# Hybrid diffusion layers on one core: the first modulation as chunks on the tensor engine, two feature tiles in turn

## The chip, the cores and the metric

One core of a Trainium2 chip runs the whole program. The metric is the device time of one execution in microseconds (us). The engines: PE (tensor engine; PEld is its weight load), DVE (vector engine), ACT (scalar engine), POOL (GpSimd) and SP, which here only issues DMAs. Each engine works through its own queue in the order in which the program was scheduled, and waits for the others by semaphores.

## What is computed

Two layers of a diffusion backbone over 512 latent tokens and 256 context tokens, width 1024. Only the beginning of the first layer matters here:

```python
sh_a, sc_a, g_a, sh_f, sc_f, g_f = jnp.split(silu_c @ mod_w[l] + mod_b[l], 6, axis=-1)
csh_a, csc_a, cg_a, csh_f, csc_f, cg_f = jnp.split(silu_cc @ mod_w[l] + mod_b[l], 6, axis=-1)
a_lat = modulate(h_lat, sh_a, sc_a)        # rms_norm(x) * (1 + scale) + shift
a_ctx = modulate(h_ctx, csh_a, csc_a)
...
p_lat = a_lat @ w_in
p_ctx = a_ctx @ w_in
```

`silu_c` belongs to the latent tokens and `silu_cc` to the context tokens; both use the same `mod_w`. After this come attention, the output product and SwiGLU of layer 0, then layer 1 and a final norm. All of it is in float32; the large products split each operand into a rounded high part and a rest, and add three products (high x high, high x rest, rest x high).

## The kernel before, in words

Activations lie feature-major: `X[k]` holds feature tile k (128 of the 1024 features, one per partition) for 768 tokens, of which `LATS` are the first 512 and `CTXS` the last 256. A scheduler with a timeline of its own sets the order of instructions on each engine; the buffers per tag (`BUFS`, `PBUFS`) say how far loads run ahead (12 of `st`, 4 each of `ph` and `pl`, 3 each of `wr`, `wh` and `wl`).

The start of the program, up to about 92 us of the profile, does this:

- It loads `X` for the latent tokens (L157, eight DMAs of the SP queue), squares it (L348, ACT), adds the squares (L351, DVE), sums them over the partitions (L365, PE), takes root and reciprocal (L367 ACT, L368 DVE) and spreads the result over the partitions (L369 DVE, L374 PE, L377 ACT). That is `rms`; `r` is its result. The context tokens go through the same lines once more.
- Component 1 (scale) of the modulation is made by PE in four chunks of 256 features, both token kinds at once (`mods_pe`): the weights arrive as four tiles of 128x512 per chunk, eight products give rows (L191), ACT copies them (L193), PE turns them into columns (L195), DVE adds the bias (L199).
- Component 0 (shift) is made tile by tile (`mod_tile`, its `dense` branch): for each of eight feature tiles two DMAs of 256 KB, two multiply-and-sum instructions by DVE for the latent tokens (L237, L241), and for the context tokens a product by POOL (L254), a sum by ACT (L255) and two small steps of DVE (L257, L258). These read the conditioning vector spread over the partitions, which `load_cond` loads (512 KB each) and puts through a SiLU on ACT (L163).
- For each feature tile, `modulate` forms x times scale times r (L399, DVE), adds the shift with rounding to the high part (L400, ACT) and forms the rest (L401, DVE). `load_start` loads the tile's weights (256 KB) and splits them (L340 ACT, L341 DVE). `start_products` (L751 to L753) adds the tile's share to six PSUM banks `ov`: four of latent tokens (three products each, so 12 matmuls) and two of context tokens (6 matmuls).
- `SCALES` says before which feature tile a chunk of the scale is made. The latent part of tile k comes first, then the context part of the tiles that are `late`.

Behind the start the banks are copied out (`put_vs`, L473 and L474), while PE goes on with the first panels of `w_in` (L316 to L318), and the modulation of component 2 runs in the background by the same `mod_tile` path.

Of the kernel before, what the change touches and what calls it, by code (L numbers as in the profile page):

```python
# [14 lines left out]
P = 128  # L15
# [34 lines left out]
NR = "nb"  # L50
PE_MODS = ((0, 1), (0, 4), (0, 5))
SCALES = (2, 0, 1, 0, 1, 0, 0, 0)
KEEP = 1
# [5 lines left out]
KC = (0, 1, 0)  # L59
C1 = 0  # L60
VP = 0
# [39 lines left out]
def hybrid_kernel(ctx: ExitStack, tc, I, out):  # L101
# [54 lines left out]
    for k in range(KT):  # L156
        dma(X[k][:, LATS], I["xc"][k, :, LATS])  # L157
    modb = const("modb", [P, 96])
# [15 lines left out]

    MOD, picks = {}, []

    dense, tile, late, first = [True], [-9], [], {}

    def mods_pe(l, comp, get):
# [4 lines left out]
        for c in range(4):  # L184
            o = get()
            for k in range(KT):
                if k % 2 == 0:
                    w = T("st", [P, 512]) if comp == 1 else T(("ph", "pl")[k // 2 % 2], [P, 512])
                    dma(w, I["mod_wp"][PE_MODS.index((l, comp)), c, k // 2])
                g = slice(32 * (k % 4), 32 * (k % 4) + 32)  # L190
                PE.matmul(o[g, :NX], cond_col[:, k], w[:, NX * (k % 2) : NX * (k % 2) + NX], start=k < 4, stop=k > 3)  # L191
            t, d = T("p", [P, NX]), get()
# [548 lines left out]
    r = B(tag="nb")  # L741
    rms(X, LATS, r, lambda: PS("t"))
    A = [(B(F32R), B(F32R)) for _ in range(KT)]
# [12 lines left out]
    def start_products(k, w, tiles):  # L756
        for t in tiles:
            three(ov[t], [x[:, t * P : (t + 1) * P] for x in A[k]], w, k == 0, k == KT - 1)

# [29 lines left out]

    scales, late = mods_pe(0, 1, PM), deque()  # L790
    for k in range(KT):
        for _ in range(SCALES[k]):
            next(scales)
        if k == 0:
            load_cond(0)
            if C1 == 0:
                load_cond(1)
        shift = mod_tile(0, 0, k, (0, 1))
        next(shift)
        modulate(A[k], X[k], k, r, 0, 0, 0, LATS)  # L800
        w = load_start(k)
        start_products(k, w, range(4))
        late.append((k, w, shift))
        if k == 0:
            if C1:
                load_cond(1)
            for x in range(KT):
                dma(X[x][:, CTXS], I["xc"][x, :, CTXS])
            rms(X, CTXS, r, lambda: PS("t"))
        while late:  # L810
            i, w, shift = late.popleft()
            next(shift)
            modulate(A[i], X[i], i, r, 0, 0, 1, CTXS)
            start_products(i, w, (4, 5))
    sel = const("sel", [4, P], F32R)
# [784 lines left out]
```

## Time and profile before

| | us |
|---|---|
| median of three runs | 1619.1 (1618.13 to 1621.35) |
| the profiled execution: its own time | 1621.04 |
| the profiled execution: span | 1619.3 |
| PE busy in the span | 1540.7 (95%) |
| DVE / ACT / POOL busy in the span | 1215.1 / 812.2 / 316.9 |
| PE busy in the first 92 us | 58.15 |
| DVE busy in the first 92 us | 74.24 |

Times in the rows are microseconds from the start of the span; a row of the timeline gives start, duration, engine, line, operation and what it writes and reads, and in brackets the idle time before it and what ended that. Rows of stretches give the stretch, its length, then busy time (and instructions) of PE, PEld, DVE, ACT and POOL, the granted PE clock (1.00 is full), the DMA engines' busy share and GB/s.

### The profile page before, as it was taken

How to read it: one execution, taken by the hardware profiler on the slowest of the kernel's cores; microseconds unless marked ns; L12 is line 12 of the kernel's file. 1: busy time of each engine (PE TensorE's matmuls, PEld its weight loads, DVE VectorE, ACT ScalarE, POOL GpSimd, SP SyncE). 2: the span in 40 equal slices, each digit the busy share in tenths (PEclk: the TensorE clock that was granted, in tenths of full speed). 3: DMA queues.
4: the chain of work that ended last, by engine and by line, in shares of the span. 5: the costliest groups of instructions: out<-in, count | busy, mean ns of one | idle time of the engine just before them, and what ended most of it. 6: DMA issues, size and time to landing. Idle time of an engine off the chain costs nothing. (4 is left out here: it accounts for less than half of the span.)

```text
span 1619.3 us, 26531 instructions
## 1 busy us (share of the span) xinstructions
PE 1540.7 (95%) x9906; PEld 1365.0 (84%) x9906; DVE 1215.1 (75%) x2438; ACT 812.2 (50%) x1652; POOL 316.9 (20%) x319
## 2 busy tenths in 40 slices
PE   4799989999998999999999999999999999999997
PEld 2577867786896999999999998787879998898997
DVE  5994868667678679596767777768877688687685
ACT  5453576677365324243333333467756554454453
POOL 1550733321000110202111112384003000000002
PEclk9999999999999999999999999999999999999998
DMA  9445232101752363646547477122005133223222
GB/s 330 160 163 169 60 118 84 36 11 28 246 196 93 114 209 124 234 153 208 200 144 270 163 254 261 60 92 79 1 1 185 50 112 122 93 92 118 91 99 85
DMA packets 77913, 214.92 MB, mean 133 GB/s; under 512 B 10196, under 2 KB 17880, under 8 KB 77784
## 3 DMA queue, kind: packets, MB, share of 16 engines
q1 hardware_dynamic: 60888, 147.16, 28.0%
q0 software_dynamic: 14592, 62.92, 11.2%
q10 hardware_dynamic: 2304, 3.15, 0.5%
q8 instruction: 78, 1.28, 0.3%
q14 instruction: 51, 0.42, 0.1%
HBM read 186.97 MB, written 23.07 MB: 130 GB/s over the span
## 5 line engine op out<-in xcount | busy, mean ns | idle before, releaser
L306 ACT CAST wh<-wr 128x1024 fp32r<-128x1024 f32 (+2 forms) x148 | 113.4, 781 | 204.1 <-PE pss L317 40.6
L307 DVE TENSOR_TENSOR wl<-wr,wh 128x1024 fp32r<-128x1024 f32 (+2 forms) x145 | 137.3, 954 | 80.2 <-ACT wh L306 79.8
L351 POOL TENSOR_TENSOR p<-p,p 128x256 f32<-128x256 f32 (+1 forms) x33 | 33.1, 1002 | 464.1 <-ACT p L348 463.1
L541 ACT ACTIVATE p<-p,sm 128x512 f32<-128x512 f32 (+3 forms) x144 | 105.1, 730 | 34.9 <-DVE sm L545 32.5
L215 DVE CUSTOM_DVE_ANT_0 p<-rope,cond 128x1024 bf16<-128x1024 f32 x64 | 77.2, 1222 | 34.1 <-DMA rope<-in_mod_w_dram 34.0
L317 PE MATMUL psd<-b,wh 128*128 128x512 f32 (+3 forms) x266 | 89.8, 339 | 0.1
L316 PE MATMUL psd<-b,wh 128*128 128x512 f32 (+3 forms) x226 | 80.1, 354 | 1.6 <-ACT b L474 1.0
L210 POOL DMA_DIRECT2D rope<-in_mod_w_dram x48 | 25.8, 537 | 284.9 <-DVE mod L215 284.9
L316 PE MATMUL pss<-st,wh 128*128 128x256 f32 (+2 forms) x233 | 79.2, 340 | 1.4 <-ACT st L1051 0.9
L535 PE MATMUL pso<-ph,b 128*64 128x256 f32 (+1 forms) x384 | 77.0, 359 | 3.3 <-DVE ph L473 3.3
L1239 PE MATMUL pss<-b,wh 128*128 128x256 f32 (+1 forms) x258 | 79.3, 307 | 0.7 <-ACT b L340 0.7
L1241 PE MATMUL pss<-b,wl 128*128 128x256 f32 (+1 forms) x258 | 79.3, 307 | 0.1
L1240 PE MATMUL pss<-b,wh 128*128 128x256 f32 (+1 forms) x258 | 79.4, 308 | 0.0
L318 PE MATMUL pss<-st,wl 128*128 128x512 f32 (+2 forms) x233 | 79.0, 339 | 0.0
L318 PE MATMUL psd<-b,wl 128*128 128x512 f32 (+3 forms) x226 | 78.3, 347 | 0.0
L535 PE MATMUL pso<-pl,b 128*64 128x256 f32 (+1 forms) x384 | 76.7, 359 | 0.2 <-DVE pl L473 0.2
L1239 PE MATMUL pst<-b,wh 128*128 128x384 f32 (+1 forms) x240 | 74.9, 312 | 0.0
L1240 PE MATMUL pst<-b,wh 128*128 128x384 f32 (+1 forms) x240 | 74.8, 312 | 0.0
L1241 PE MATMUL pst<-b,wl 128*128 128x384 f32 (+1 forms) x240 | 74.3, 311 | 0.0
L317 PE MATMUL pss<-b,wh 128*128 128x256 f32 (+3 forms) x228 | 73.2, 323 | 0.3 <-DVE b L1227 0.2
L1240 PE MATMUL psd<-b,wh 128*128 128x384 f32 (+1 forms) x222 | 69.8, 314 | 0.3 <-DVE b L341 0.3
L1239 PE MATMUL psd<-b,wh 128*128 128x384 f32 (+1 forms) x222 | 69.6, 314 | 0.0
(548 smaller groups left out, 5496.9 us busy)
## 6 DMA issues: line engine op xcount, KB each, us to landing
wr<-in_w_gu_dram SPq DMA_DIRECT2D x88, 512.0 KB, 3.9
rope<-in_mod_w_dram POOLq DMA_DIRECT2D x48, 512.0 KB, 3.8
wr<-in_w_out_dram SPq DMA_DIRECT2D x32, 512.0 KB, 3.6
wr<-in_w_dn_dram SPq DMA_DIRECT2D x64, 256.0 KB, 3.0
p<-home POOLq DMA_DIRECT2D x40, 384.0 KB, 5.3
home<-p POOLq DMA_DIRECT2D x40, 384.0 KB, 4.2
wr<-in_w_in_dram SPq DMA_DIRECT2D x21, 512.0 KB, 3.5
ph<-in_mod_w_dram SPq DMA_DIRECT2D x24, 256.0 KB, 3.4
```

The costliest lines, as they stand in the source:

```text
L215: V.tensor_tensor_reduce(out=T("p", [P, D], mybir.dt.bfloat16), in0=w, in1=cond[:, v, :], op0=ALU.mult, op1=ALU.add, scale=1.0, scalar=0.0 ...
L306: behind(S.copy(h, r), *after[:1])
L307: behind((G if eng else V).tensor_tensor(lo, r, f(h), op=ALU.subtract), *after[1:])
L316: PE.matmul(o, wh[:, k], mh[:, c], start=first and k == 0, stop=False)
L317: PE.matmul(o, wh[:, k], ml[:, c], start=False, stop=False)
L318: PE.matmul(o, wl[:, k], mh[:, c], start=False, stop=last and k == n - 1)
L351: marks["add"] = (eng or V).tensor_tensor(acc[:, :n], acc[:, :n], t[:, :n], op=ALU.add)
L535: ins = PE.matmul(o[64 * i : 64 * i + 64, c], v(kt), t, start=n == 0, stop=n == len(moving[i]) - 1)
L541: S.activation(p[:, c], p[:, c], AF.Exp, bias=nm, scale=-1.0, accum_out=dn)
L1239: PE.matmul(o, wh, xh, start=first and k == 0, stop=False, skip_group_check=not first)
L1240: PE.matmul(o, wh, xl, start=False, stop=False, skip_group_check=not first)
L1241: PE.matmul(o, wl, xh, start=False, stop=k == 3, skip_group_check=not first)
```

## The change

- Component 0 of layer 0 joins the components that PE makes in chunks, for both token kinds (`PE_MODS`). Its weights come from the chunk layout; chunks of scale and shift alternate (`first_mods`), two feature tiles per chunk pair. The per-tile work of DVE, POOL and ACT for this component is gone.
- `X` is loaded by the SP and the ACT queue in turn.
- The squares of the latent `X` are six by ACT and two by DVE; they are added in pairs, and PE adds the four pair sums (16 instructions instead of 4 at the line `sum`).
- The first tiles of `w_start` are split ahead of the loop. In the loop, the latent products of two tiles come first, then the next chunk of scale and of shift (held behind those products by `chunk_after`), then the context products of the two tiles. The context norm stands behind the second chunk pair.
- The context half of `X` is loaded in two groups of four; `load_cond` comes with the third pair.

```diff
--- before.py
+++ after.py
@@ -48,8 +48,7 @@
 QF = 0
 LQ, EACH = 50, 0
 NR = "nb"
-PE_MODS = ((0, 1), (0, 4), (0, 5))
-SCALES = (2, 0, 1, 0, 1, 0, 0, 0)
+PE_MODS = ((0, 1), (0, 0), (0, 4), (0, 5))
 KEEP = 1
 OUTQ = 1
 E1, EF = 1, 1
@@ -57,7 +56,6 @@
 AFTER = "012k5678"
 DBG = 0.38
 KC = (0, 1, 0)
-C1 = 0
 VP = 0
 TURN1, MANY = (0,), 0
 RK, RQ, RL, SQ = (2, 0), (0, 0), (0, 0), 1
@@ -154,7 +152,7 @@
     cond = T("cond", [P, 2, D])
     X = [B() for _ in range(KT)]
     for k in range(KT):
-        dma(X[k][:, LATS], I["xc"][k, :, LATS])
+        (nc.sync, nc.scalar)[k % 2].dma_start(X[k][:, LATS], I["xc"][k, :, LATS])
     modb = const("modb", [P, 96])
     ident_r = const("ident", [P, P], F32R)
 
@@ -172,7 +170,7 @@
     S.activation(cond_col, cond_col, AF.Silu)
 
 
-    MOD, picks = {}, []
+    MOD, picks, chunk_after = {}, [], []
 
     dense, tile, late, first = [True], [-9], [], {}
 
@@ -188,7 +186,8 @@
                     w = T("st", [P, 512]) if comp == 1 else T(("ph", "pl")[k // 2 % 2], [P, 512])
                     dma(w, I["mod_wp"][PE_MODS.index((l, comp)), c, k // 2])
                 g = slice(32 * (k % 4), 32 * (k % 4) + 32)
-                PE.matmul(o[g, :NX], cond_col[:, k], w[:, NX * (k % 2) : NX * (k % 2) + NX], start=k < 4, stop=k > 3)
+                behind(PE.matmul(o[g, :NX], cond_col[:, k], w[:, NX * (k % 2) : NX * (k % 2) + NX], start=k < 4, stop=k > 3),
+                       *chunk_after)
             t, d = T("p", [P, NX]), get()
             S.copy(t, o[:, :NX])
             for m in range(2):
@@ -739,7 +738,17 @@
 
 
     r = B(tag="nb")
-    rms(X, LATS, r, lambda: PS("t"))
+    squares = []
+    for k in range(KT):
+        t = B(tag="p")
+        if k in (5, 7):
+            V.tensor_tensor(t[:, LATS], X[k][:, LATS], X[k][:, LATS], op=ALU.mult)
+        else:
+            S.activation(t[:, LATS], X[k][:, LATS], AF.Square)
+        if k % 2:
+            V.tensor_tensor(t[:, LATS], t[:, LATS], squares[-1][:, LATS], op=ALU.add)
+        squares.append(t)
+    rstd(squares[1::2], D, LATS, r, lambda: PS("t"))
     A = [(B(F32R), B(F32R)) for _ in range(KT)]
 
     def load_start(k):
@@ -755,7 +764,8 @@
 
     def start_products(k, w, tiles):
         for t in tiles:
-            three(ov[t], [x[:, t * P : (t + 1) * P] for x in A[k]], w, k == 0, k == KT - 1)
+            ins = three(ov[t], [x[:, t * P : (t + 1) * P] for x in A[k]], w, k == 0, k == KT - 1)
+        return ins
 
     def project(src, use, cols=(LATS, CTXS), m=P, every=2, eng=None, w=None, get=PQ):
 
@@ -787,31 +797,35 @@
         turn[0] += 1
         return PS("ot"[turn[0] % 2])
 
-    scales, late = mods_pe(0, 1, PM), deque()
-    for k in range(KT):
-        for _ in range(SCALES[k]):
-            next(scales)
-        if k == 0:
-            load_cond(0)
-            if C1 == 0:
-                load_cond(1)
-        shift = mod_tile(0, 0, k, (0, 1))
-        next(shift)
-        modulate(A[k], X[k], k, r, 0, 0, 0, LATS)
-        w = load_start(k)
-        start_products(k, w, range(4))
-        late.append((k, w, shift))
-        if k == 0:
-            if C1:
-                load_cond(1)
-            for x in range(KT):
-                dma(X[x][:, CTXS], I["xc"][x, :, CTXS])
+    late = deque()
+    first_mods = [mods_pe(0, comp, PM) for comp in (1, 0)]
+
+    for g in first_mods:
+        next(g)
+    starts = [load_start(k) for k in range(2)]
+    for c in range(0, KT, 2):
+        for k in (c, c + 1):
+            modulate(A[k], X[k], k, r, 0, 0, 0, LATS)
+            gate = [start_products(k, starts[k], range(4))]
+        chunk_after[:] = gate
+        for i, g in enumerate(first_mods if c + 2 < KT else ()):
+            if c == 0:
+                for x in range(4 * i, 4 * i + 4):
+                    dma(X[x][:, CTXS], I["xc"][x, :, CTXS])
+            next(g)
+            if c + i == 0:
+                starts.extend(load_start(k) for k in (2, 3))
+        if c == 0:
             rms(X, CTXS, r, lambda: PS("t"))
-        while late:
-            i, w, shift = late.popleft()
-            next(shift)
-            modulate(A[i], X[i], i, r, 0, 0, 1, CTXS)
-            start_products(i, w, (4, 5))
+        elif c + 2 < KT:
+            starts.extend(load_start(k) for k in (c + 2, c + 3))
+        for k in (c, c + 1):
+            modulate(A[k], X[k], k, r, 0, 0, 1, CTXS)
+            start_products(k, starts[k], (4, 5))
+        if c == 4:
+            for v in range(2):
+                load_cond(v)
+    chunk_after.clear()
     sel = const("sel", [4, P], F32R)
     VN = [B() for _ in range(4)]
     sets = [(new_q(), new_k()) for _ in range(2)]
```

The lines of the changed kernel are shifted against those of the kernel before (by one or two lines up to the loop, by 9 or 14 behind). What stands in the queues now, at three places:

First, ACT at the norm of the latent tokens. `b_68` to `b_75` are the eight tiles of `X`, `pst` a bank, `sm` the small tile of the norm, `nb_97` is `r`, `wr`/`wh` are a tile of `w_start` and its high part. Before:

```order
L348 ACTIVATE p_118<-b_75 128x512
L147 CAST ident_r_88<-nb_86 128x128
L367 ACT_TABLE_LOAD
L367 ACTIVATE sm_122<-pst_121,eps_90 128x4
L377 COPY nb_97<-pst_131 128x512
L163 ACT_TABLE_LOAD
L163 ACTIVATE cond_67<-cond_67 128x1024
L193 COPY p_175<-pst_158 128x256
L163 ACTIVATE cond_67<-cond_67 128x1024
L193 COPY p_199<-pst_182 128x256
L340 CAST wh_227<-wr_225 128x512
```

With the change:

```order
L747 ACTIVATE p_108<-b_72 128x512
L747 ACTIVATE p_113<-b_74 128x512
L145 CAST ident_r_88<-nb_86 128x128
L339 CAST wh_219<-wr_217 128x512
L339 CAST wh_225<-wr_223 128x512
L366 ACT_TABLE_LOAD
L366 ACTIVATE sm_119<-pst_118,eps_90 128x4
L376 COPY nb_97<-pst_140 128x512
L339 CAST wh_291<-wr_289 128x512
L192 COPY p_184<-pst_167 128x256
L192 COPY p_210<-pst_193 128x256
```

Two casts of `w_start` now stand ahead of the root (`sm`) of the norm, one more behind it, and the two SiLUs of `cond` are gone from this place.

Second, ACT at the norm of the context tokens. Before:

```order
L348 ACTIVATE p_259<-b_71 128x256
L348 ACTIVATE p_262<-b_72 128x256
L255 ACTIVATE pl_216,part_288<-pl_216 128x512
L348 ACTIVATE p_265<-b_73 128x256
L348 ACTIVATE p_268<-b_74 128x256
L348 ACTIVATE p_271<-b_75 128x256
L340 CAST wh_318<-wr_316 128x512
L367 ACT_TABLE_LOAD
L367 ACTIVATE sm_275<-pst_274,eps_90 128x2
L340 CAST wh_391<-wr_389 128x512
L377 COPY nb_97<-pst_282 128x256
L400 ACTIVATE b_134<-p_293,mod_70_211 128x256
```

With the change (`p_322` is the copied row of the second chunk of the shift; `p_322` and `p_329` are different tiles of one tag):

```order
L192 COPY p_322<-pst_305 128x256
L347 ACTIVATE p_329<-b_68 128x256
L347 ACTIVATE p_331<-b_69 128x256
L347 ACTIVATE p_334<-b_70 128x256
L347 ACTIVATE p_337<-b_71 128x256
L347 ACTIVATE p_340<-b_72 128x256
L347 ACTIVATE p_343<-b_73 128x256
L347 ACTIVATE p_346<-b_74 128x256
L161 ACT_TABLE_LOAD
L161 ACTIVATE cond_67<-cond_67 128x1024
L347 ACTIVATE p_349<-b_75 128x256
L161 ACTIVATE cond_67<-cond_67 128x1024
```

All eight squares are now behind the copy of the second shift chunk. A table load and both SiLUs of `cond` stand ahead of the root of the norm, and behind these rows follow the cast of `sel`, a second table load, the root itself and the copy to `r`.

Third, PE around the third chunk pair (`pss`, `pst_162` are banks of latent tokens, `psd` of context tokens, `pst_439` of the shift chunk). With the change:

```order
L761 MATMUL pst_162<-wl_298,b_149 128x512
L762 MATMUL pst_162<-wh_297,b_150 128x512
L194 MATMUL pso_433<-pick_64,p_432 128x2 x2
L189 MATMUL pst_439<-ph_440,cond_col_63 32x256 x2
L189 MATMUL pst_439<-pl_444,cond_col_63 32x256 x2
L189 MATMUL pst_439<-ph_448,cond_col_63 32x256 x2
L189 MATMUL pst_439<-pl_452,cond_col_63 32x256 x2
L194 MATMUL pso_457<-pick_64,p_456 128x2 x2
L760 MATMUL psd_163<-wh_291,b_147 128x512
L761 MATMUL psd_163<-wl_292,b_147 128x512
L760 MATMUL psd_164<-wh_291,b_147 128x512
```

The chunk pair ends (the last row of `pick_64`) and the context products of the third feature tile (`b_147`) follow directly behind it. In the kernel before no shift stands on PE, and the context products of a tile follow the latent products of the next tile.

## Prediction

> **What bounds the kernel now.** I read the stretches first, to see which engine is full where.
>
> ```profile
> 0.00:92.00 92.00, 58.15 (x263) 40.93 (x264) 74.24 (x152) 49.15 (x108) 37.56 (x28) 0.93 0.70 237
> 92.00:140.00 48.00, 46.97 (x291) 40.56 (x289) 37.86 (x78) 26.11 (x58) 14.95 (x10) 1.00 0.44 141
> 80.00:90.00 10.00, 7.84 (x32) 5.53 (x31) 10.00 (x20) 4.61 (x13) 6.70 (x5) 1.00 0.57 193
> ```
>
> In the first 92 us PE (first number behind the length) is busy for 58 of 92 us; from 92 us on it is full. DVE (third number) is busy for 74 us, and in the last of these stretches it has no idle time at all. The change touches only this start, so I ask by how much the moment moves at which PE becomes full. That moment is read from these rows of the timeline:
>
> ```profile
> 26.09 0.80 PE L751 MATMUL pss<-wh,b 128*128 128x512 f32 x1 [3.02 <-ACT b L400]
> 81.08 0.39 PE L316 MATMUL pst<-b,wh 128*128 128x512 f32 x1
> 81.31 0.39 PE L317 MATMUL pst<-b,wh 128*128 128x512 f32 x1
> 91.41 0.61 PE L753 MATMUL psd<-wh,b 128*128 128x512 f32 x2
> 92.31 0.28 PE L316 MATMUL pss<-b,wh 128*128 128x256 f32 x1
> ```
>
> The first product starts at 26.09. Matmuls of 512 columns follow each other at 0.23 us (81.08 to 81.31). The last product of the start begins at 91.41, but the first panel of `w_in` (24 matmuls on `pst`) has run in its gaps since 81.08, so at 92.31 PE is past 144 products of the start and these 24. 92.31 is the mark that I compare.
>
> The longest wait of PE for another engine's products up to 95 us (sum, times, longest), and the costliest groups of DVE and POOL up to 110 us (busy, mean ns of one, idle before them):
>
> ```profile
> PE pss L753 <- DVE b L401: 6.2, 5, 1.6
> L237 DVE CUSTOM_DVE_ANT_0 p<-pl,cond,mod 128x512 bf16<-128x512 f32 x15 | 13.2, 878 | 0.1
> L254 POOL TENSOR_TENSOR ph<-ph,cond 128x512 f32<-128x512 f32 x15 | 24.9, 1659 | 38.5 <-ACT cond L163 21.1 <-DVE mod L237 14.2 <-DVE mod L199 1.2
> ```
>
> PE waits for the results of `modulate` (L400 in the row at 26.09, L401 here), which stand on DVE among the shift's sums. Taking the shift off DVE and POOL (16 of the 30 L237 and 16 of the 30 L254 in these groups and their twins) therefore removes the wait that holds PE now. The question is what comes late in its place.
>
> **The first norm and the first product.** ACT will hold two casts of `w_start` ahead of the norm's root. They wait for their tiles, which SP issues behind x, 48 and 64 KB of constants and eight modulation tiles. Bytes up to the second one: 18 times 256 KB, and 128, 48 and 64 KB, about 4.97 MB.
>
> ```profile
> 0.00:10.00 10.00, 0.00 (x0) 0.00 (x0) 2.99 (x6) 5.64 (x9) 0.32 (x5) 1.00 0.77 251
> 10.00:20.00 10.00, 6.31 (x42) 3.38 (x42) 2.94 (x5) 5.14 (x8) 0.00 (x0) 1.00 1.03 373
> 20.00:30.00 10.00, 5.55 (x23) 4.51 (x20) 8.78 (x22) 8.93 (x20) 3.35 (x2) 0.66 0.98 315
> 30.00:40.00 10.00, 5.61 (x51) 3.48 (x49) 7.59 (x15) 3.57 (x10) 3.23 (x2) 1.00 1.05 380
> 12.40 1.86 PE L365 MATMUL pst<-ones,p 128*128 128x1 f32 x8 [12.40 <-DVE p L351]
> 14.30 0.27 ACT L367 ACTIVATE sm<-pst,eps 128x4 f32<-128x4 f32 x1 [1.61 <-PE pst L365]
> 15.55 2.08 PE L374 MATMUL pst<-p,ones 128*128 128x512 f32 x2 [1.29 <-DVE p L369]
> 17.56 2.56 PE L191 MATMUL pst<-st,cond_col 128*32 128x256 f32 x32
> L340 ACT CAST wh<-wr 128x512 fp32r<-128x512 f32 x8 | 4.9, 612 | 2.5 <-DMA wr<-in_w_start_dram 1.6 <-PE psd L753 0.8
> ```
>
> The DMA engines move 2.51 MB by 10 us and are full from there at 373 GB/s, so the second tile lands at 10 + 2.46/0.373 = 16.6. Then cast 0.61 and table load 1.28 (a row below): 18.5, where the root stands at 14.30 now. From root to spread takes 1.25 (14.30 to 15.55), spread and two chunks run to 20.12 as now (4.57): 24.3. The new path then goes through PE's columns, a bias step, two tiles of scale, a bias step and ACT:
>
> ```profile
> 36.58 0.50 PE L195 MATMUL pso<-pick,p 128*128 128x2 f32 x4
> L199 DVE SCALAR_TENSOR_TENSOR mod<-pso,modb 128x2 f32<-128x2 f32 x8 | 1.0, 149 | 0.2 <-PE pso L195 0.2
> 50.73 0.74 DVE L401 SCALAR_TENSOR_TENSOR b<-p,mod,b 128x512 fp32r<-128x512 f32 x1
> 34.01 0.48 DVE L399 SCALAR_TENSOR_TENSOR p<-b,mod,nb 128x256 f32<-128x256 f32 x1
> L399 DVE SCALAR_TENSOR_TENSOR p<-b,mod,nb 128x256 f32<-128x256 f32 x8 | 11.0, 1374 | 0.0
> L400 ACT ACTIVATE b<-p,mod 128x512 fp32r<-128x512 f32 x8 | 5.8, 722 | 11.5 <-DVE mod L241 11.5
> L400 ACT ACTIVATE b<-p,mod 128x256 fp32r<-128x256 f32 x8 | 4.0, 501 | 5.9 <-DVE mod L258 5.0 <-DVE p L399 0.9
> ```
>
> The L399 of 256 columns takes 0.48 alone, and 1.37 in the mean of all eight, most of which overlap a product of POOL. POOL now stands idle until component 2 begins, so I take the short durations: 0.74 for 512 columns, as L401 at 50.73, which has the same operands' sizes, and 0.48 for 256. The sum is 0.5 + 0.3 + 1.5 + 0.3 + 0.7 and a tenth for handing on: first product at **27.7**, against 26.09. With stretched steps on DVE it would be 29, the upper end.
>
> Two edits I cost at nothing here. Two queues for x: the engines are full from about 5 us on, and the casts above wait for later bytes; without them ACT would have the root at about 16.4, since PE now adds four pair sums, 32 of its entries instead of 8 at 0.23 us from about 10 us on. So without this cover the edit would still be late by 2 us. The earlier add of squares is hidden in the same way.
>
> **Two tiles and the second chunk pair.** 24 matmuls at 0.23 us, of which the first run at half clock:
>
> ```profile
> 46.00:48.00 2.00, 0.79 (x2) 0.69 (x3) 2.00 (x5) 1.26 (x3) 0.10 (x1) 0.55 0.29 108
> 50.00:52.00 2.00, 2.00 (x6) 1.59 (x5) 2.00 (x8) 1.12 (x3) 1.12 (x1) 0.50 0.00 0
> 52.00:54.00 2.00, 2.00 (x8) 1.55 (x7) 2.00 (x6) 1.34 (x3) 0.72 (x2) 0.75 0.46 131
> 28.00:30.00 2.00, 2.00 (x8) 1.63 (x7) 1.76 (x6) 1.97 (x3) 0.00 (x0) 0.72 0.99 367
> 37.01 1.11 PE L191 MATMUL pst<-st,cond_col 128*32 128x256 f32 x16
> L193 ACT COPY p<-pst 128x256 f32<-128x256 f32 x4 | 1.4, 361 | 0.2 <-DVE mod L237 0.2
> ```
>
> The granted clock is about 0.5 from some 23 to 28.7 and from 46.5 to 53, each time until PE has been busy for 2.6 and 5.8 us. I take 3 us here: it holds 7 matmuls at twice 0.23, and 17 at 0.23 follow, 6.9 in all: 34.6. A chunk is 1.1 (L191), a copy 0.36, columns 0.5; two chunks in turn end at 38.6, the second copy at **38.1**.
>
> **The context norm.** Behind that copy ACT does everything that the context products need:
>
> ```profile
> 27.17 1.02 ACT L348 ACTIVATE p<-b 128x256 f32<-128x256 f32 x3
> 28.71 1.28 ACT L367 ACT_TABLE_LOAD   x1
> 19.57 1.06 ACT L163 ACTIVATE cond<-cond 128x1024 f32<-128x1024 f32 x1
> 30.87 0.26 ACT L367 ACTIVATE sm<-pst,eps 128x2 f32<-128x2 f32 x1 [0.88 <-PE pst L365]
> 33.27 0.37 ACT L377 COPY nb<-pst 128x256 f32<-128x256 f32 x1
> ```
>
> Eight squares 2.8, two table loads 2.6, two SiLUs 2.1, a cast 0.3, the root 0.26: 46.2. (The second `cond` has 13.35 MB ahead of and in it and lands at 40.4; the squares behind it wait for it only if it is later than 42.) Root to copy end is 2.77 now (30.87 to 33.64) with a cast in the way; I take 1.8, then 0.5 DVE and 0.5 ACT: first context product at **49.0**. PE waits from 38.6 with about 1.2 of work in between: this is the new wait. Queued behind it on PE are the latent products of the third and fourth tile.
>
> **The rest.** From 49.0: 120 products at 0.23, 27.6; four chunks with columns, 4 x 1.6 = 6.4; copies that PE waits for, 1.2; half clock at the restart, 4.3 us as a value between 2.6 and 5.8, costs 2.2. After the third and fourth chunk pair PE goes straight to context products, whose inputs need a bias step, four or six DVE instructions (two of 0.74, the others 0.48; behind the fourth pair also one L237 of 0.8), a second bias step and 0.5 on ACT, begun 2.1 us before the pair ends: 0.3 + 2.44 + 0.3 + 0.5 - 2.1 = 1.45, and by the same sum with 3.4 and 0.8 in place of 2.44, 3.2. Together 4.6. Total 42.0: 91.0. Then the 24 matmuls of the first `w_in` panel, 5.5: **96.5**. DVE does not delay them: per pair it has four scale and four rest steps of each size's half, 4.9, two rests of weights, 1.4, and bias steps, 0.6, about 7 us beside PE's 36 x 0.23 + 3.2 = 11.5.
>
> **Sum.** 96.5 - 92.3 = +4.2 us. The profiled execution took 1621.04, so 1625.2 for it; it lay 1.9 above the median of 1619.1, so by the median **1623.3**. POOL's relief is worth nothing on PE beyond this, and the removed DMAs of 4.2 MB come back as chunk tiles of the same bytes.
>
> On the clock, "TensorE: Matmul & The Clock Gate", section "Part 1: The HAM clock gate", in the Trainium skill has the clock halved after an idle window of about 3.4 us and restored after as long a busy one. The rows agree with the fall, less with the return (5.8 us). By that rule the restart at 49.0 would cost 1.7 instead of 2.2, and the sum would be +3.7.
>
> **Rivals.**
> 1. *Absorbed later* (not slower). After the start DVE's background work stands at the same time as now, so waits of PE for DVE behind it may not move along. Between 190 and 310 us the largest are:
>
> ```profile
> PE pss L735 <- DVE sm L545: 4.7, 5, 1.7
> ```
>
> If DVE sets these at its own time, 4.2 of the 4.7 us go and the time is 1619. It decides if DVE enters that stage no later than now. Against it: DVE's inputs there come from PE's products, which are full from 92 to 190. Chance 0.22.
> 2. *The low ends.* No half clock (-1.6 and -2.2), the root bound by PE's sums (-2), context gaps of 1.5 instead of 4.6: -8.9, so 1614.5. For it: POOL no longer stretches DVE. Against it: the half clock came after every long idle stretch. Chance 0.18.
> 3. *Late banks.* Behind the start the bank for the second `w_in` product has to be copied out by DVE, which stands behind eleven L237 of component 2:
>
> ```profile
> 98.81 0.68 DVE L237 CUSTOM_DVE_ANT_0 p<-ph,cond 128x512 bf16<-128x512 f32 x1
> ```
>
> The eleventh such L237 now ends at 99.5. With fewer copies ahead and a start 2 us sooner I put the copy at 95.6, just in time. If it comes at 102 instead, PE waits 6 us more: 1629. Chance 0.20.
> 4. That the change does not do what it says (x no sooner, shift still on DVE) the queues exclude for the shift; for x it costs nothing, as said.
>
> **How the numbers follow.** Forecast 0.40, rivals 0.22, 0.18, 0.20. The forecast's own range, from no half clock at the restart (-2.2) and a first norm 1.6 sooner to a stretched first product (+1.3) and 5.8 us of half clock at both starts (+2.2), is 1619.5 to 1627. With the rivals I take 1614.5 to 1630, which leaves out the outer halves of rivals 2 and 3. A difference of 0.2%, 3.2 us, is about what a measurement of this kernel can tell from none: faster below 1615.9, slower above 1622.3. The forecast gives slower 0.29 and same 0.11, rival 1 same 0.18 and faster 0.04, rival 2 faster 0.14 and same 0.04, rival 3 slower: 0.18, 0.33, 0.49.
>
> **What would show it.** Right: root of the first norm near 18.5, first product near 27.7, PE idle from about 38 to 49 with ACT busy on squares, table load and SiLU; gaps of 1.5 and 3 us behind the third and fourth chunk pair; first 256-column product of `w_in` near 96.5. Wrong: `w_start` landing before 14; context products before 45; PE waiting for a bank at 97; a mark near 96 with an unchanged total.

## The result and the profile after

The changed kernel takes 1638.2 us in the median (1636.8 to 1639.9), against 1619.6 for the kernel before: the ratio is 1.0119, with a 95% interval of 1.0104 to 1.0133. That is +18.6 us where I had +4.2, and above my range. The direction held, the size did not.

These are the stretches of the kernel after (length, then busy time of PE, PEld, DVE, ACT and POOL with instruction counts, granted clock of PE, DMA share, GB/s):

```profile
0.00:92.00 92.00, 63.24 (x335) 44.73 (x335) 40.09 (x88) 35.19 (x68) 7.17 (x10) 0.91 0.64 220
92.00:140.00 48.00, 42.90 (x220) 37.15 (x221) 41.75 (x89) 26.28 (x60) 19.61 (x12) 0.93 0.45 142
80.00:90.00 10.00, 8.79 (x38) 6.58 (x36) 10.00 (x21) 5.66 (x12) 5.55 (x4) 1.00 0.61 205
90.00:100.00 10.00, 6.38 (x28) 4.94 (x28) 10.00 (x19) 4.73 (x13) 7.45 (x5) 1.00 0.55 181
100.00:110.00 10.00, 6.62 (x31) 5.96 (x30) 10.00 (x29) 4.91 (x15) 5.56 (x5) 0.73 0.57 170
```

In the first 92 us PE is even busier than before (63 against 58 us), and DVE has lost almost half of its work (40 against 74). What is new lies behind: from 90 to 110 PE is busy for only 13 of 20 us, at a clock that falls to 0.73 in the last ten. Before, PE was full from 92 us on. DVE has not one idle moment from 80 to 110, but that alone is not new; in the kernel before it was busy for 29.8 of these 30 us:

```profile
80.00:110.00 30.00, 26.81 (x136) 21.75 (x135) 29.81 (x64) 15.65 (x42) 19.47 (x12) 1.00 0.53 177
```

The timeline of PE after (start, length, what, and in brackets the idle time before it with its releaser) has the places that I had named:

```profile
29.14 0.50 PE L760 MATMUL pss<-wh,b 128*128 128x512 f32 x1 [1.54 <-ACT b L399]
...
51.86 0.80 PE L760 MATMUL psd<-wh,b 128*128 128x512 f32 x1 [1.52 <-ACT b L399]
...
91.92 0.50 PE L761 MATMUL pss<-wl,b 128*128 128x512 f32 x1 [1.90 <-DVE wl L340]
...
96.65 0.50 PE L317 MATMUL pst<-b,wl 128*128 128x512 f32 x1 [1.72 <-DVE wl L306]
...
105.33 0.58 PE L315 MATMUL pss<-b,wh 128*128 128x256 f32 x1 [3.38 <-ACT b L473]
```

First product 29.14 (I had 27.7), first context product 51.86 (49.0), and the mark, the first 256-column product of `w_in`, 105.33 (96.5; before 92.31). The last three rows are new waits: for the low part of the last `w_start` tile, for that of the first `w_in` tile, and for a bank.

ACT ahead of the two roots:

```profile
16.50 1.31 ACT L339 CAST wh<-wr 128x512 fp32r<-128x512 f32 x2 [6.49 <-DMA wr<-in_w_start_dram]
17.84 1.28 ACT L366 ACT_TABLE_LOAD   x1
19.13 0.26 ACT L366 ACTIVATE sm<-pst,eps 128x4 f32<-128x4 f32 x1
...
40.71 2.25 ACT L347 ACTIVATE p<-b 128x256 f32<-128x256 f32 x7
42.98 1.28 ACT L161 ACT_TABLE_LOAD   x1
44.27 1.06 ACT L161 ACTIVATE cond<-cond 128x1024 f32<-128x1024 f32 x1
45.23 0.40 ACT L347 ACTIVATE p<-b 128x256 f32<-128x256 f32 x1
45.54 1.04 ACT L161 ACTIVATE cond<-cond 128x1024 f32<-128x1024 f32 x1
46.49 0.28 ACT L145 CAST sel_r<-nb 4x128 fp32r<-4x128 f32 x1
46.78 1.28 ACT L366 ACT_TABLE_LOAD   x1
48.08 0.26 ACT L366 ACTIVATE sm<-pst,eps 128x2 f32<-128x2 f32 x1
```

The first root waits behind two casts, the second behind squares, two table loads, two SiLUs and a cast, both as predicted; the first root begins 0.6 us later than predicted (19.13 against 18.5), the second ends 2.1 later (48.34 against 46.2).

The lag is the start of a product of `w_in` in one kernel less the start of the same product in the kernel before. It is 14.3 us at the product that started at 110.51 before, and stays there to 170. So three quarters of the loss are made in the first 110 us. Up to 780 us of the kernel before it lies mostly between 14.0 and 15.5; it then grows in steps to 19.6 by 1180, and is 19.4 at the last of these products (the spans differ by 18.9). One execution of run 7 below, at 5283 us, counts in its median but not in its ratio.

### The profile page after: what moved, and what is told of

It reads as the page before. It is cut to its first block, busy times and chain, and to the rows that moved or that the text cites. A ratio compares the mean times of both kernels' runs of the same rounds, so it can differ in the third digit from the quotient of the medians.

```text
span 1638.2 us, 26608 instructions
## 1 busy us (share of the span) xinstructions
PE 1557.8 (95%) x10010; PEld 1378.5 (84%) x10010; DVE 1184.8 (72%) x2389; ACT 800.2 (49%) x1622; POOL 291.4 (18%) x303
## 5 line engine op out<-in xcount | busy, mean ns | idle before, releaser
L306 DVE TENSOR_TENSOR wl<-wr,wh 128x1024 fp32r<-128x1024 f32 (+2 forms) x145 | 135.8, 944 | 86.0 <-ACT wh L305 85.5
L315 PE MATMUL psd<-b,wh 128*128 128x512 f32 (+3 forms) x226 | 80.3, 355 | 1.7 <-ACT b L440 1.3
```

The costliest lines, as they stand in the source:

```text
L306: behind((G if eng else V).tensor_tensor(lo, r, f(h), op=ALU.subtract), *after[1:])
L315: PE.matmul(o, wh[:, k], mh[:, c], start=first and k == 0, stop=False)
```

## The experiments

Two sets of theories were put up. On the place: **A**, ACT's order ahead of the two roots makes the loss and passes it down; **B**, DVE's unbroken work from 80 us on makes it; **C** in the first four runs, the added matmuls of the chunks do; **D**, the edits on x; **E**, the order by two tiles itself. Later, **C** is the rival that work held back costs as much where it goes. On the mechanism in the stretch, from 80 to 110 us: **P**, POOL's products slow DVE, and **Q**, DVE's own sums take places in its queue. All times in one table; the ratio is taken with the runs of the kernel before on the same chip (medians 1619.3 to 1620.6), the three starts are those of the profiled execution:

| kernel | median us | ratio to before, 95% | first product | first context product | mark |
|---|---|---|---|---|---|
| before | 1619.6 | 1 | 26.09 | 35.08 | 92.31 |
| after | 1638.2 | 1.0104 to 1.0133 | 29.14 | 51.86 | 105.33 |
| 1 SiLUs late | 1634.0 | 1.0053 to 1.0109 | 28.25 | 47.71 | 100.42 |
| 2 context norm first | 1631.6 | 1.0052 to 1.0086 | 30.61 | 48.67 | 103.80 |
| 3 root first | 1634.6 | 1.0065 to 1.0107 | 27.11 | 50.63 | 108.23 |
| 4 before, shift by PE | 1621.6 | 0.9990 to 1.0019 | 24.81 | 36.08 | 89.50 |
| 5 hold, as written | 1642.5 | 1.0134 to 1.0166 | 29.29 | 51.72 | 104.88 |
| 6 x undone | 1630.3 | 1.0059 to 1.0086 | 23.38 | 45.22 | 102.59 |
| 7 as 4, with x | 1622.6 | 0.9999 to 1.0028 | 30.77 | 38.91 | 91.55 |
| 8 as 4, hold as written | 1624.9 | 1.0026 to 1.0052 | 25.16 | 37.35 | 91.44 |
| 9 true hold | 1623.0 | 1.0010 to 1.0032 | 29.59 | 52.32 | 97.50 |
| 10 as 4, true hold | 1612.7 | 0.9940 to 0.9972 | 24.98 | 37.21 | 86.73 |
| 11 edits 1, 2, 6 | 1626.1 | 1.0022 to 1.0053 | 24.47 | 40.27 | 99.08 |
| 12 as 11, true hold | 1616.5 | 0.9967 to 0.9992 | 24.39 | 40.40 | 86.73 |
| 13 POOL cut | 1629.4 | 1.0033 to 1.0071 | 28.70 | 52.50 | 98.68 |
| 14 DVE cut | 1634.2 | 1.0047 to 1.0100 | 29.51 | 52.08 | 103.01 |
| 15 before, true hold | 1614.7 | 0.9945 to 0.9975 | 25.91 | 34.85 | 87.76 |
| 16 as 6, true hold | 1621.7 | 0.9992 to 1.0020 | 24.54 | 46.62 | 92.02 |

### Runs 1 to 3: ACT's queue ahead of the roots

Run 1 holds the SiLUs back:

```diff
-        S.activation(cond[:, v, :], cond[:, v, :], AF.Silu)
+        behind(S.activation(cond[:, v, :], cond[:, v, :], AF.Silu), *chunk_after)
```

> The changed kernel with one edit: the two SiLUs of the conditioning tiles are held behind the last product ahead of the chunk pair, so that they no longer stand on ACT between the context squares and the context root, and the table loads between them go too. Theory A (the loss is made by what ACT does ahead of the context norm's root, and passes down the line): the first context product moves from 51.9 us to about 47.3 (two SiLUs of 1.27 and two table loads of 1.2 to 1.3 us less), and the time falls by 4 to 5 us, to about 1633.5. Theory B (the stretch from 80 to 105 us, in which DVE is busy without a gap with component 2, sets the start of the wide products whatever happens ahead of it): the first context product moves as well, but the first 256-column product stays within 1 us of 105.3 and the time within 1.5 us of 1638.2. Theory C (the added chunk matmuls on PE are the loss): no change beyond 1 us, and no move of what follows.

Run 2 moves the context loads and norm ahead of the second chunk pair:

```diff
         chunk_after[:] = gate
+        if c == 0:
+            for x in range(KT):
+                dma(X[x][:, CTXS], I["xc"][x, :, CTXS])
+            rms(X, CTXS, r, lambda: PS("t"))
...
-            if c == 0:
-                for x in range(4 * i, 4 * i + 4):
-                    dma(X[x][:, CTXS], I["xc"][x, :, CTXS])
...
-        if c == 0:
-            rms(X, CTXS, r, lambda: PS("t"))
```

> The changed kernel with one edit: the context columns of x are loaded, and their norm is computed, ahead of the second chunk pair's matmuls in the program, so that ACT squares them before it copies the second pair of shift and scale. Theory A (ACT's order ahead of the context root is what costs): the idle stretch of PE between 41 and 51.9 us shrinks by 8 to 10 us, the first context product starts at 42 to 44, and the time falls by 7 to 9 us, to about 1630. Theory B (DVE's unbroken work from 80 to 105 us binds): the first context product moves as well, but the first 256-column product moves by under 3 us from 105.3, and the time falls by under 3 us. Theory C (the added chunk matmuls): under 1 us.

Run 3 holds two casts behind the root:

```diff
-    starts = [load_start(k) for k in range(2)]
+    starts, root = [], marks["root"]
+    for k in range(2):
+        starts.append(load_start(k))
+        behind(marks["cast"], root)
```

> The changed kernel with one edit: the casts of the first two w_in start tiles are held behind the root of the first norm on ACT. Theory A: the root moves from 19.1 to about 17.8 us, the first product from 29.1 to about 27.7, and the time falls by about 1.4 us, to 1636.8, unless the wait for the context norm, which is set by ACT's own chain, swallows it (then 0). Theory B: 0, since the tail absorbs it. Theory C: 0.

Run 1 came out as A expects: first context product at 47.71, the time 4.2 us lower, the mark 4.9 sooner. But its four executions lie between 1627.9 and 1637.8 us, and the starts are those of the fastest. Run 2 gained its 6.6 us, but not by its stated path: the first context product stood at 48.67 and not at 42 to 44. ACT's timeline in run 2:

```profile
40.40 0.37 ACT L376 COPY nb<-pst 128x256 f32<-128x256 f32 x1 [1.51 <-PE pst L373]
40.79 1.28 ACT L161 ACT_TABLE_LOAD   x1
42.09 2.00 ACT L161 ACTIVATE cond<-cond 128x1024 f32<-128x1024 f32 x2
43.99 0.35 ACT L192 COPY p<-pst 128x256 f32<-128x256 f32 x1
```

The norm is done at 40.77, but the SiLUs now stand ahead of the copy of the second scale chunk. And in run 3:

```profile
17.52 0.26 ACT L366 ACTIVATE sm<-pst,eps 128x4 f32<-128x4 f32 x1 [6.08 <-PE pst L364]
```

The root now waits for PE's 32 column sums instead of the casts (my prediction had 16.4 for this case), and the first product moves to 27.11; yet the mark came later (108.23). Its 3.6 us in the median therefore don't come from the start, and I take differences of this size, the 4.2 of run 1 too, between these kernels, whose later order shifts, as not settled. So A holds for a part, and the mark stays 8 us or more behind that of the kernel before in each: something else stands ahead of it.

### Runs 4, 6 and 7: one part alone, one part undone

Run 4 gives the kernel before the chunks for the shift, and nothing else (the per-tile shift of the loop goes with it):

```diff
-PE_MODS = ((0, 1), (0, 4), (0, 5))
-SCALES = (2, 0, 1, 0, 1, 0, 0, 0)
+PE_MODS = ((0, 1), (0, 0), (0, 4), (0, 5))
+SCALES = (1, 1, 0, 1, 0, 1, 0, 0)
...
-    scales, late = mods_pe(0, 1, PM), deque()
+    chunks, late = [mods_pe(0, comp, PM) for comp in (1, 0)], deque()
```

> The kernel before with one edit alone: the shift of the first modulation comes from chunks of matmuls on PE, as its scale does, in the loop order of before, with x by one queue, the conditioning tiles loaded early and the norm's squares as before. Theory A (the new order is the loss, the move of the shift to PE is not): the time stays between 1614 and 1624 us: 4 chunks at about 1.6 us of PE are 6.4 us more on PE, against 16 vector products of the shift that no longer hold DVE back. Theory B (DVE's backlog of component 2 from 80 us on is the loss, and it is there because products reach the tail later): DVE has less to do in the first 90 us, so the first 256-column product comes no later than 92.3 plus 2. Theory C (the chunks on PE are the loss): 1630 or more.

Run 6 takes the two hunks on x out of the changed kernel (one queue, `rms(X, LATS, ...)` as before):

> The changed kernel with one edit undone: x comes by one queue again, and the norm sums all eight squares into one tile, of which PE takes 8 column sums instead of 32 of four pair sums. In the changed kernel PE's 32 entries end at 17.44, 5.8 us behind the last pair sum of DVE at 11.7; before they end at 14.26, 1.9 us behind DVE's last sum at 12.35. But the two casts of start weights stay ahead of the root on ACT, with the second tile landing near 16.5. Theory A: root at 18 to 19 in either, so first product within 0.8 us of 29.1 and the time within 1.5 us of 1638.2. Theory D (the two edits on x are themselves a good part of the loss): root below 17, first product below 27.5, and the time lower by 2 us or more.

Run 7 puts these two hunks into run 4:

> The kernel before with the shift from PE chunks (as in the run that gave 1621.6) and with the two edits on x as well (two queues, pair sums), in the loop order of before. Theory A (the turn order of chunks, latent and context products is the loss): within 3 us of 1621.6; PE's sums end later by 3 us, and as the first product hangs on the root alone here, it starts 2 to 3 us later, and the time is up to 3 us longer. Theory D (the edits on x are a good part of the loss): 1626 or more.

Run 4 ends theory C: 1621.6 us, no difference that can be told from the kernel before. In the old order the exchange of DVE's work for PE's costs nothing in sum; what costs is where things stand. The edits on x cost about 1 us in the old order, which can't be told from nothing (run 7, in which the first product is 6 us later than in run 4 and the mark 2), and 8 us in the new one (run 6). Run 6 came out as D had it, not A: without the two edits on x the casts fell behind the root by themselves, so the root came at 14.15 and not at 18 to 19, as ACT's timeline of run 6 shows:

```profile
14.15 0.26 ACT L366 ACTIVATE sm<-pst,eps 128x4 f32<-128x4 f32 x1 [1.63 <-PE pst L364]
17.52 0.58 ACT L376 COPY nb<-pst 128x512 f32<-128x512 f32 x1 [3.11 <-PE pst L373]
18.00 1.14 ACT L339 CAST wh<-wr 128x512 fp32r<-128x512 f32 x2
```

The edits on x are what put the casts ahead; which of the two did it was not tried.

### Runs 5, 8, 9, 10, 15: component 2 held back

Run 5 starts the background sums of component 2 later in the program, run 8 does the same to run 4:

```diff
+    held = lambda i: max(0, (i - 24) // 2)
...
-        bg(int(i * DBG) - int(i * DBG - DBG))
+        bg(held(i) - held(i - 1))
```

> The changed kernel with one edit: the background sums of component 2 (on DVE, POOL and ACT) begin 24 steps of the wide products later, and then go at a rate of one in two steps, so that the same 36 pieces are done by the end of the projections. Theory B (DVE, busy without a gap from 80 us on, holds the last splits of weights and the copies out of the banks): PE's waits of 1.9, 1.7 and 3.4 us ahead of the first 256-column product go, that product starts at 97 to 99 instead of 105.3, and the time falls by 5 to 7 us. Theory A (only what stands ahead of the first context product counts): the first 256-column product comes sooner by under 2 us, the time by under 2. Rival C (the held pieces are late for the stage behind and cost there what they save here): the first 256-column product at 97 to 99, and the time within 2 us of 1638.

> The kernel before with the shift from PE chunks, and the background sums of component 2 held back by 24 steps of the wide products. With the shift on PE alone, PE waited 5.6 us for a bank that ACT had not copied out, while DVE and POOL did component 2. Theory B (component 2's sums crowd the end of the start): the wait of 5.6 us goes, the first 256-column product starts at 84 to 86 instead of 89.5, and the time is 1616 to 1617, faster than before by 3 us. Rival C (the held pieces cost in the stage behind what they save here): 1620 to 1623.

These two didn't do what they say: on DVE the same number of L236 stood in nearly the same places from 80.3 us on (eleven up to 106 us in run 5 as in the changed kernel). It looks as if the scheduler takes an instruction as soon as its tiles are there, wherever it is written. Both kernels became slower, by 4.3 and 3.3 us; why is not shown. Runs 9 (on the changed kernel), 10 (on run 4) and 15 (on the kernel before) tie the sums and products on DVE and POOL to the last product of the first `w_in` panel, and spread them evenly from there on:

```diff
-                    V.tensor_tensor_reduce(...)
+                    behind(V.tensor_tensor_reduce(...), *held)
...
-                    G.tensor_tensor(w, w, cond[:, 1, c], op=ALU.mult)
+                    behind(G.tensor_tensor(w, w, cond[:, 1, c], op=ALU.mult), *held)
...
+    units = lambda i: max(0, (i - 8) * 36 // 88)
...
+        if i == 8:
+            held[:] = [marks["wide"]]
+        bg(units(i) - units(i - 1))
```

> The changed kernel with one edit: the sums of component 2 on DVE and POOL are ordered behind the last product of the first panel of wide products, so that none of them runs before it (in the earlier try they were only written later in the program, and the scheduler put as many of them in the same places). Theory B (component 2's work on DVE and POOL between 80 and 105 us costs PE its waits there): the waits of 1.9, 1.7 and 3.4 us shrink to under 2.5 in all, the split of 1024 columns takes about 1.1 us instead of 2.2, the first 256-column product starts at 98 to 100 instead of 105.3, and the time is 4 to 7 us lower, near 1632. Rival C (the work costs as much where it goes): first 256-column product at 98 to 100, and the time 1636 or more. Theory A (only what stands ahead of the first context product counts): first 256-column product at 103 or later.

> The kernel before with the shift from PE chunks and the same true hold of component 2. Theory B: the wait of 5.6 us for a bank goes to under 1, the first 256-column product starts at 84 to 86 instead of 89.5, and the time is near 1617, 4 to 5 us below that kernel without the hold (1621.6). Rival C: 1620 to 1624.

> The kernel before with the same true hold of component 2. If the change made the stretch (DVE free of the shift, so that component 2 meets the last modulates, splits and copies), the kernel before gains little: PE's waits there for weights and banks are 1.1 and 1.0 us, and the time is 1617 to 1620. If the stretch costs as much in the kernel before, the time is 1612 or less.

The stretches of run 9:

```profile
80.00:90.00 10.00, 9.41 (x42) 7.49 (x42) 6.94 (x14) 5.20 (x9) 0.00 (x0) 1.00 0.61 208
90.00:100.00 10.00, 10.00 (x55) 8.70 (x54) 7.28 (x24) 4.30 (x12) 1.36 (x2) 1.00 0.47 145
100.00:110.00 10.00, 10.00 (x59) 8.82 (x58) 9.87 (x17) 5.45 (x14) 7.91 (x5) 1.00 0.51 157
```

With POOL idle from 80 to 90, PE is full from 90 on, the three waits are gone, the clock stays whole, the mark is 97.50 and the time 1623.0: the hold alone takes away 15.2 of 18.6 us, with a head (what stands ahead of the stretch) as late as in the changed kernel. Theory B holds, with over twice the gain that I had put on it, and the rival that the work costs the same elsewhere falls. Run 10 gains 8.9 us against run 4, and run 15 lies between its two cases: the kernel before pays this toll too, only less, 4.9 us (1619.6 to 1614.7). Both are faster than the kernel before, and between them (1612.7 and 1614.7) the intervals overlap. A table of four:

| | mark | mark with hold | us | us with hold |
|---|---|---|---|---|
| before | 92.31 | 87.76 | 1619.6 | 1614.7 |
| after | 105.33 | 97.50 | 1638.2 | 1623.0 |

So of the 18.6 us, 8.3 stay when both are held (1623.0 against 1614.7); the start up to the mark, which is 9.7 later, is the likely place. The other 10.3 are a larger toll of component 2's early work (15.2 against 4.9).

### Runs 13 and 14: how the stretch costs

```diff
-        at, ts, one = l * 48 + comp * 8 + m, {}, float(comp in (1, 4))
+        at, ts, one, x = l * 48 + comp * 8 + m, {}, float(comp in (1, 4)), slice(0, 16 if (l, comp) == (0, 2) else 512)
...
-                    G.tensor_tensor(w, w, cond[:, 1, c], op=ALU.mult)
+                    G.tensor_tensor(w[:, x], w[:, x], cond[:, 1, c][:, x], op=ALU.mult)
```

Run 13 is this, POOL's products on 16 of 512 columns; run 14 cuts the operands of `V.tensor_tensor_reduce` in the same way and leaves POOL's. Both leave out work and give a wrong gate of the first block.

> The changed kernel, in which POOL's products of component 2 take 16 of their 512 columns (work is left out: the gate of the first block is wrong for the context), while DVE's sums, ACT's accumulations and their places in the queues stay. Theory P (POOL's products slow DVE's instructions beside them, and DVE waits in its queue for what comes from them): the split of 1024 columns falls from 2.2 to about 1.1 us, L400 from 1.08 to about 0.57, the first 256-column product starts at 98 to 100 instead of 105.3, and the time is 8 us or more lower. Theory Q (DVE's own sums take places ahead of modulates, splits and copies): the first 256-column product gains under 3 us, and the time under 5.

> The changed kernel, in which DVE's sums of component 2 take 16 of their 512 columns (work is left out: the gate of the first block is wrong for the latents), while POOL's products stay whole. Theory Q (DVE's own sums take places ahead of modulates, splits and copies, eleven of 0.74 to 0.86 us between 80 and 106): the first 256-column product starts 5 us or more sooner and the time is 5 us or more lower. Theory P (POOL's products beside DVE's work cost most): the first 256-column product gains under 4 us, the split of 1024 columns still takes 2.2 us.

DVE's groups between 80 and 106 us in the changed kernel (busy, mean ns of one, idle before them):

```profile
L306 DVE TENSOR_TENSOR wl<-wr,wh 128x1024 fp32r<-128x1024 f32 x2 | 4.4, 2196 | 0.0
L400 DVE SCALAR_TENSOR_TENSOR b<-p,mod,b 128x512 fp32r<-128x512 f32 x2 | 2.5, 1253 | 0.0
L257 DVE SCALAR_TENSOR_TENSOR mod<-mod,modb 128x1 f32<-128x1 f32 x2 | 2.5, 1234 | 0.0
L472 DVE COPY b<-pss 128x128 f32<-128x128 f32 x7 | 1.8, 277 | 0.0
```

and in run 13, where POOL's products are cut:

```profile
L306 DVE TENSOR_TENSOR wl<-wr,wh 128x1024 fp32r<-128x1024 f32 x4 | 4.9, 1225 | 0.0
L472 DVE COPY b<-pss 128x128 f32<-128x128 f32 x8 | 2.0, 278 | 0.0
L400 DVE SCALAR_TENSOR_TENSOR b<-p,mod,b 128x512 fp32r<-128x512 f32 x2 | 1.5, 748 | 0.0
L257 DVE SCALAR_TENSOR_TENSOR mod<-mod,modb 128x1 f32<-128x1 f32 x5 | 0.7, 149 | 0.0
```

A step on one column takes 1.23 us beside POOL and 0.15 without it; the copies out of banks take 0.28 in both. With DVE's queue nearly in the same order, the mark moves to 98.68, the lag at 110 us from 14.3 to 4.9, and the time by 8.8 us. Run 14, with DVE's sums cut to 16 columns and POOL whole, moves the mark by 2.3 and the time by 4.0; its splits of 1024 columns still take up to 2.3. Theory P is the larger part, Q the smaller. The timelines of DVE and POOL of the changed kernel show the single event:

```profile
94.30 2.29 DVE L306 TENSOR_TENSOR wl<-wr,wh 128x1024 fp32r<-128x1024 f32 x1
96.51 1.24 DVE L257 SCALAR_TENSOR_TENSOR mod<-mod,modb 128x1 f32<-128x1 f32 x1
97.67 0.15 DVE L256 TENSOR_TENSOR mod<-part,part 128x1 f32<-128x1 f32 x1
```

```profile
93.90 1.61 POOL L253 TENSOR_TENSOR pl<-pl,cond 128x512 f32<-128x512 f32 x1 [0.89 <-DVE mod L236]
95.47 2.26 POOL L253 TENSOR_TENSOR ph<-ph,cond 128x512 f32<-128x512 f32 x1
```

POOL's first product ends at 95.51. DVE's split, begun at 94.30, takes another 1.08 us from there to its end at 96.59, nearly the whole 1.23 that it takes in run 13. POOL's second product then stretches to 2.26 and ends at 97.73, and the one-column step, begun at 96.51, ends at 97.75. Going by these ends, each waits for the other to finish, instruction by instruction. In the Trainium skill, "SBUF — State Buffer", section "Who interferes with whom", has this as an exclusive lock on a port pair that DVE (with two inputs in SBUF) and GpSimd share, in which the later one blocks fully; these rows agree with it, and the copies out of banks, which have no such inputs, are not touched. They still come late when such instructions stand ahead of them in DVE's queue. PE's longest wait, the 3.38 ahead of the mark, ends with the copy by ACT in the last row here; that one waited for a copy of DVE, which stood behind the split, the one-column step and two sums L236:

```profile
99.30 2.10 DVE L306 TENSOR_TENSOR wl<-wr,wh 128x1024 fp32r<-128x1024 f32 x1
101.33 1.23 DVE L257 SCALAR_TENSOR_TENSOR mod<-mod,modb 128x1 f32<-128x1 f32 x1
105.01 0.27 ACT L473 COPY b<-pss 128x128 f32<-128x128 f32 x1 [0.91 <-DVE b L472]
```

### Runs 11, 12 and 16: what is left of the head

Run 11 joins the edits of runs 1, 2 and 6; run 12 is run 11 with the true hold, run 16 is run 6 with it.

> The changed kernel with three edits together: x by one queue with the norm as before, the context norm's squares ahead of the second chunk pair, and the two SiLUs held behind the products ahead of the chunk pair. What is left of the change is the shift on PE and the order of chunks, latent and context products by two tiles. Theory A (ACT's order ahead of the two roots makes the loss): the single gains of 7.9, 6.6 and 4.2 us overlap in part; first context product near 37 to 39, and the time 1620 to 1624. Theory E (the order by two tiles has a loss of its own, since each chunk pair, its copies and its modulates stand in one chain with PE's products): 1625 or more, with PE waiting over 5 us in all behind the chunk pairs.

> The same as the run of the order alone, with the true hold of component 2. Theory B: 4 to 7 us below that run, 1616 to 1619, no slower than the kernel before. Rival C: within 2 us of that run.

> The changed kernel with the true hold and with the edits on x undone. First root at 14.2 instead of 19.1. If a start sooner by 5 us passes down when nothing holds PE behind it, the time is 4 to 6 us below the run with the hold alone (1623.0), 1617 to 1619; with ctx squares and SiLUs moved as well it was 1616.5, so that these two would be worth under 3. If the chain of the context norm takes it up: 1621 to 1623.

Run 11 is slower than A expected (1626.1, the figure of E), but not for E's reason: PE's waits for the copied rows of the chunks are 3.0 us in all, not over 5. Its waits of PE up to 115 us (sum, times, longest) hold two of the stretch:

```profile
PE pst L317 <- DVE wl L306: 4.8, 1, 4.8
...
PE pss L315 <- DVE b L472: 2.2, 1, 2.2
```

Run 12, with the hold, has neither and is at 1616.5, 9.5 us lower, its mark at 86.73 like that of run 10. So with ACT's order and the stretch both mended, the order by two tiles is within 2 us of the kernel before with the hold (1614.7). Run 16 gains 5.5 us at the mark against run 9 and only 1.4 in the median; its lag grows by 4 us between 170 us and the end of its profiled execution, and I can't say whether that is more than the spread of single executions.

Put side by side, the toll of component 2's early work is 4.9 us in the kernel before, 8.9 with the shift on PE in the old order (runs 4 and 10), 9.5 and 8.7 in the order by two tiles without the edits on x (11 and 12, 6 and 16), and 15.2 with them (after and 9). So, as far as these medians tell, the order by two tiles hardly adds to it; the chunks of the shift and the edits on x do. Of the 8 us that the edits on x cost in the new order, only 1.4 are left with the hold. How a later first norm makes the toll larger is not shown.

## Why the prediction was wrong

- *First norm and first product.* The mechanism was right: the root behind two casts. It came at 19.13 and not 18.5, because both casts ran from 16.50 on, where I had one left by then. The first product came at 29.14 against 27.7: the spread and the two chunks behind it took 5.6 us (20.39 to about 26.0) and not 4.57. The term "edits I cost at nothing" was wrong in a way that the casts hid: run 6 shows that the two edits on x brought the casts there, and that they cost 8 us in this order.
- *Two tiles and context norm.* My 6.9 for the 24 matmuls is 7.1 by its own figures, which changes nothing. The rest was right in its parts: PE was idle from 41.5 to 51.9 but for the norm's sums and its spread, and the first context product was 2.9 us later than I had it.
- *The gaps of 4.6 behind the third and fourth chunk pair* did not come; the context products behind a pair use shift and scale of the chunks made a pair earlier. In PE's timeline after they follow the pairs directly:

```profile
65.77 0.61 PE L194 MATMUL pso<-pick,p 128*128 128x2 f32 x4 [0.57 <-ACT p L192]
66.27 0.50 PE L760 MATMUL psd<-wh,b 128*128 128x512 f32 x1
...
79.14 0.61 PE L194 MATMUL pso<-pick,p 128*128 128x2 f32 x4 [0.52 <-ACT p L192]
79.61 0.48 PE L760 MATMUL psd<-wh,b 128*128 128x512 f32 x1
```

Only a wait of 1.2 us stands further on, so 3.4 of the 4.6 fell away. This offsets the 2.9 above, and it is luck.
- *Half clock at the restart.* The stretch after has it for 4 us, worth 2.0 against the 2.2 taken:

```profile
52.00:56.00 4.00, 4.00 (x10) 3.14 (x11) 3.11 (x6) 1.60 (x3) 0.00 (x0) 0.50 0.00 0
```

- ***"DVE does not delay them"* is the step that failed.** I counted DVE's work of the last pairs at short durations and left component 2 out of it. In the order by two tiles the last pair's scale and rest steps (L398, L400) come behind the last chunk pair, and component 2 (L236) begins in their midst:

```profile
78.20 2.59 DVE L398 SCALAR_TENSOR_TENSOR p<-b,mod,nb 128x256 f32<-128x256 f32 x5
80.71 0.68 DVE L236 CUSTOM_DVE_ANT_0 p<-ph,cond 128x512 bf16<-128x512 f32 x1
...
84.57 3.19 DVE L400 SCALAR_TENSOR_TENSOR b<-p,mod,b 128x512 fp32r<-128x512 f32 x2
```

The last row counts a step of 512 columns and one of 256 together; I had them at 0.74 and 0.48, and they take 3.19. Run 9, in which that work is held back, has its mark at 97.50 and its time at 1623.0, next to the 96.5 and 1623.3 of my sum, though the sum comes so near only because two misses in it cancel. What the sum lacked is component 2 in this stretch: 7.8 us at the mark, 10.6 by 110 us (14.3 less 3.7), where the products behind run at a clock of 0.73, and 15.2 in the time; the 4.6 between the last two come later.
- *Rival 3* named the right work, component 2 ahead of what PE waits for, and gave it one bank and 6 us. It was three waits, and the price came from POOL more than from the queue.
- *Rival 1* fell: the waits between 190 and 310 us moved along. The profile after has

```profile
PE pss L734 <- DVE sm L544: 4.8, 5, 1.7
```

where the kernel before had 4.7 in as many waits.
- *"POOL's relief is worth nothing on PE beyond this"* was asked of the wrong half: the removed products brought nothing that run 4 could show, but those that are left now stand beside work that PE waits for, and cutting them brought 8.8 us (run 13).

That the chunks cost little was right: run 4 shows no difference. The last 4.6 us of the loss (18.9 in the spans less 14.3) come behind 780 us of the kernel before, in a few steps, and their cause stays open. From 780 to 1180 us the lag grows by 5.7 here, by 1.6 in run 9, 2.1 in run 14 and 5.8 in run 13.

## What to carry to other kernels

When a change makes a stretch idle on one engine, look where its background work now lands: it starts when its tiles are there, and here it met the last steps that the next stage waits for. Price an instruction of DVE with two inputs in SBUF beside a product of POOL as the sum of both, not the longer, and hold background work behind a named instruction rather than by its place in the program.

## What the runs showed of the hardware that was not expected

A DVE step on 128x1 elements can take 1.24 us, when a POOL product of 128x512 runs beside it (0.15 without). Between 80 and 106 us this and the longer splits and scale steps added 9 us of DVE time: the groups L306, L400, L257, L256 and L236 at their means in the changed kernel less those in run 13. The kernel before, with component 2 held back, is itself 5 us faster.
